# A norm's sums of squares gathered partly by accumulating transfers, and one gate tile from another ring

## The chip, the core and the metric

The kernel runs on one core of one Trainium2 chip. The metric is the device time of one execution in microseconds (us). The engines are named as in the profile: PE multiplies matrices (PEld is its weight load), DVE works elementwise on VectorE, ACT is ScalarE, POOL is GpSimd, which computes nothing here and only issues transfers that add to what lies at the target, and SP issues nearly all other transfers. Each engine runs its instructions in one fixed order and waits on semaphores; an instruction that waits holds up all that stand behind it.

## The reference, cut to what matters

One layer on 1024 tokens of width 1024: a half-weighted SwiGLU, a token mixer with two branches, an output projection, a second half-weighted SwiGLU, a last norm.

```python
h = x + 0.5 * swiglu(rmsnorm(x, norm_ffn1), ffn1_w_in, ffn1_w_out)
proj = rmsnorm(h, norm_mix) @ w_in          # q, k, v, g_ret, p, gates
ret = rms_per_head(retention(q, k, v)) * silu(g_ret)
pool = multiscale_pool(p, pool_w, pool_scale)
gate = sigmoid(gates + gate_bias)
merged = gate[0] * (ret @ w_ret_up) + gate[1] * (pool @ w_pool_up)
h = h + merged @ w_out
h = h + 0.5 * swiglu(rmsnorm(h, norm_ffn2), ffn2_w_in, ffn2_w_out)
return rmsnorm(h, norm_final)
```

The change concerns the sum of h * h over the channels that `rmsnorm(h, norm_ffn2)` needs, and the gates of the pooling branch.

## The kernel before, in words

Activations lie transposed, 128 channels by 1024 tokens in a tile, so that a channel tile `mt` runs from 0 to 7 and a token half `j` from 0 to 1. Each matrix product is done by Strassen's scheme with seven block products (`strassen`, L478), and every operand is split into a high and a low part (`split`, L163): ACT casts the high part (L164), DVE subtracts it (L165), and a block product is three matmuls per 128 channels, high by high (L184), high by low (L185) and low by high (L186). Weights get their parts the same way. So DVE and ACT prepare what PE eats.

Two groups of output tiles run side by side (`two_by_two`, L706), in the order of blocks `BY_OPERAND`: L11 R11, L12 R21, S2 T2, S3 T3, S1 T1, L22 T4, S4 R22. In such a group the product L11 R11 goes to bank `a`; ACT copies `a` to bank `b` (L529) before the second product may go on top of `a` and S2 T2 on top of `b`. These two copies gate PE at the start of each pair of groups.

The stages around the change are: `pool_up` (the pooled branch's up projection, names `pu`, gates `pg`), `two_groups` (the retention branch's, names `ru`, result in operands `mg`), `out_group` (the output projection, names `wo`, with the groups 0 and 1 first and 2 and 3 after them), and the second SwiGLU's input product `ffn_in` (names `c`; its operands are `n3`, made from the results of `out_group`). What PE does not need at once is put on a list, `flow`, of which each step of PE takes two entries; the compiler's scheduler then fixes the order on each engine, with the evacuations of banks (`with soon()`) ahead.

An output tile of `wo` has four quarters. Two of them get the old value of h by an accumulating transfer from POOL (`onto`, L142, called at L1877) after a copy from the bank; the others get it on DVE (L1880, L1882). When a quarter is done, `Next.quarter` (L315) stores it and calls `Norm.square` (L293): ACT squares 128x512 values into a `c2` tile `n3q` (L291), and DVE adds it to `n3ssq` (L303). There are 16 quarters; the first of each token half is squared straight into `n3ssq`, so there are 14 such additions. Then `stats` (L448) has PE sum `n3ssq` over the channels, and the inverse root is made and spread.

`handed` (L1887) says which operand of the next product is made after which block: `f[5]` is the part R22, `f[1]` T2, `f[3]` T3. After the last block of the second pair the rest, for tiles 2 and 3, is put on the list.

SBUF tiles come from rings: `raw` has 4 buffers (weights as loaded, and the pooled gates `pg0` to `pg6`), `tl` 4, `c2` 8 half tiles, `wt` 5 (split weights). A new tile waits until the last reader of its buffer is done; a load waits so on SP, with all later loads behind it.

Of the kernel before, what the change touches and what calls it, by code (L numbers as in the profile page):

```python
# [15 lines left out]
ADD, SUB, MUL = ALU.add, ALU.subtract, ALU.mult  # L16
# [4 lines left out]
KT = D // P  # L21
# [32 lines left out]
BY_OPERAND = (0, 4, 1, 3, 2, 6, 5)  # L54
# [36 lines left out]
def block_kernel(ctx: ExitStack, tc, x, x_tok, x_two, vecs, f1_in, f1_out, w_in, w_v, pool_w, w_ret, w_pool, w_o,  # L91
# [3 lines left out]
    tt = nc.vector.tensor_tensor  # L95
# [4 lines left out]
    flow = Flow()  # L100
# [19 lines left out]
    def raw(name):  # L120
        return sb.tile([P, S], F32, tag="raw", bufs=N_RAW, name=name)

    def tl(name):
        return sb.tile([P, S], F32, tag="tl", bufs=N_TL, name=name)

    def t4(name):
        return sb.tile([P, S], F32, tag="t4", bufs=N_T4, name=name)

    def c2(name):
        return sb.tile([P, H], F32, tag="c2", bufs=N_C2, name=name)  # L130
# [8 lines left out]
    def load(dst, src):  # L139
        nc.sync.dma_start(dst, src)  # L140

    def onto(dst, src):  # L142
        nc.gpsimd.dma_start(dst, src, accum_op=ADD)
# [5 lines left out]
    def spill(name, n, width=S):  # L149
        return [dr.tile([P, width], F32, tag=f"{name}{i}", name=f"{name}{i}") for i in range(n)]  # L150

    def half(t, j):
        return t[:, j * H : (j + 1) * H]
# [126 lines left out]
    class Norm:  # L280


        turns = False

        def __init__(self, name):
            self.name, self.ssq, self.seen = name, None, set()
# [6 lines left out]
        def square(self, mt, tokens, src):  # L293
            if self.ssq is None:
                self.ssq = t4(f"{self.name}ssq")
            dst = self.ssq[:, tokens]
            if tokens.start not in self.seen:
                self.squared(dst, src)
                self.seen.update(range(tokens.start, tokens.stop, HD))
            else:  # L300
                q = c2(f"{self.name}q{mt}_{tokens.start}")[:, : tokens.stop - tokens.start]
                self.squared(q, src)
                tt(dst, dst, q, ADD)  # L303

    class Next(Norm):

        turns = True
# [398 lines left out]
    def two_by_two(groups, order, between=None):  # L706

        groups = list(groups)
        for z in range(0, len(groups), 2):
            pair = [g() for g in groups[z : z + 2]]  # L710
            for n in order:
                a, b = (steps[n] for steps in pair)
                yield a

                def both(b=b, z=z, n=n):
                    b[1]()
                    if between:
                        between(z // 2, n)

                yield b[0], both  # L720


    def plain(M, nk, src, name, evac, begin, banks):

        t = {}
        for q in range(0, nk, 4):

            def prep(q=q):
                if q == 0:
                    t["raw"] = raw(f"{name}raw")  # L730
                    load(t["raw"][:, : nk * P], src)
                t[q] = weights(t["raw"][:, q * P : (q + 4) * P], f"{name}w{q}")
                if q + 4 == nk:
                    begin()

            def body(q=q):
                if q == 0:
                    t["dst"] = [f(f"{name}d{j}") for j, f in enumerate(banks)]
                for i in range(4):
                    w = parts(t[q], i)  # L740
                    m = [moving(M(q + i)[j]) for j in range(2)]
                    first, final = q + i == 0, q + i == nk - 1
                    for j in range(2):
                        mm(t["dst"][j], w[0], m[j][0], start=first, stop=False)
                        mm(t["dst"][j], w[0], m[j][1], start=False, stop=False)
                    for j in range(2):
                        mm(t["dst"][j], w[1], m[j][0], start=False, stop=final)
                if q + 4 == nk:
                    evac(t["dst"])

            yield prep, body
# [434 lines left out]
    def await_stored(*names):  # L1186
        flow.until(lambda: stored.issuperset(names))
# [283 lines left out]
    def pool_up():  # L1471
        gate, stores = {}, {}
        for mt in range(KT):

            def begin(mt=mt):
                await_stored(f"t{(KT + mt) // 2}")
                if mt < KT - 1:
                    r = raw(f"pg{mt}")
                    load(r, gates[KT + mt])
                    gate[mt] = [half(r, j) for j in range(2)]  # L1480
                    stores[mt] = [(pm[mt], r)]
                    return
                gate[mt] = [c2(f"pg{mt}{j}") for j in range(2)]
                for j, g in enumerate(gate[mt]):
                    load(g, half(gates[KT + mt], j))
                stores[mt] = [(half(pm[mt], j), g) for j, g in enumerate(gate[mt])]

            def evac(dst, mt=mt):
                for j, g in enumerate(gate.pop(mt)):
                    tt(g, dst[j], g, MUL)  # L1490
                for to, at in stores.pop(mt):
                    load(to, at)

            yield from plain(M.get, KT, w_pool[mt], f"pu{mt}", evac, begin,
                             (sum_bank, sum_bank if mt < 4 else bank))
# [304 lines left out]
    def after(nx):  # L1800

        def t2(i):
            if i not in nx.t1s:
                nx.r22(i)
            nx.t2(i)

        return {0: nx.r11, 4: nx.r21, 1: t2, 3: nx.t3, 2: nx.t1, 6: nx.t4_, 5: nx.p22}
# [43 lines left out]

        return [group(n, i) for n, i in enumerate(at)]

    waiting = []

    def out_group(i):
        pair = [None, None]
        name = f"wo{i}"

        def begin():  # L1860
            for z in range(2):
                pair[z] = t4(f"{name}{z}")
                if i > 1 or z == 0:
                    load(half(pair[z], 1 - z), half(h1[i + 4 * z], 1 - z))
                else:
                    load(pair[z], h1[i + 4 * z])

        def evac(which, in0, in1):
            tile, j = which
            dst = half(pair[tile], j)  # L1870
            step = lambda: ffn2.quarter(i + 4 * tile, slice(j * H, (j + 1) * H), pair[tile])
            if tile == j and (i > 1 or tile == 0):
                if in1 is not None:
                    tt(dst, in0, in1, ADD)
                else:
                    copy(dst, in0)
                onto(dst, half(h1[i + 4 * tile], j))  # L1877
                waiting.append(step)
                return
            tt(dst, in0, dst, ADD)  # L1880
            if in1 is not None:
                tt(dst, dst, in1, ADD)  # L1882
            flow.add(step)

        return lambda: strassen(mg, w_o[i], w_o[i + 4], name, evac, none, begin)

    def handed(nx, last):  # L1887

        f = after(nx)

        def between(pair, n):
            if n in (3, 5):
                flow.add(*waiting)
                waiting.clear()
            if pair == 0:
                if n == BY_OPERAND[-1]:
                    flow.add(*(lambda m=m, i=i: m(i) for i in range(2) for m in (nx.r22, nx.sum1, nx.sum3)))
                return
            flow.add(*(lambda i=i: f[n](i) for i in range(2)))

            for m in {3: (0,), 6: (4,)}.get(n, ()):
                flow.add(*(lambda i=i: f[m](i) for i in range(2, 4)))
            if n == BY_OPERAND[-1]:
                rest = [lambda m=m, i=i: f[m](i) for m in (1, 3, 2, 6, 5) for i in range(2, 4)]
                last(rest)

        return between

    def merge():
        yield from two_by_two(two_groups(0) + two_groups(1), BY_OPERAND, handed(mg, lambda rest: flow.add(*rest)))  # L1910
        yield from two_by_two((out_group(i) for i in range(4)), BY_OPERAND,
                              handed(ffn2, lambda rest: (flow.add(*rest[:4]), ffn2.stats(between=rest[4:]))))

    ffn2 = Next("n3", V_FFN2, h2)
    ops2 = spill("r2", FH), spill("t2", FH), spill("b2", FH), spill("m2", FH, H)

    class Last(Norm):


        tiles, rows, banks, sums = {}, {}, {}, {}  # L1920
# [87 lines left out]
    def second():  # L2008
        for n, step in enumerate(ffn_in(ffn2, f2_in, ops2, "c", lambda: fetch_rows(f2_out, "d"))):
            flow.rate = 1  # L2010
            yield step
        flow.rate = 2
    flow.run(chain(ffn1(), projections(), retention(), merge(), second(),
                   ffn_out(ffn2, ops2, ops_done.setdefault("c", set()), f2_out, h2, "d", fin.quarter, fin.end, fetched, fin, f2_far)))
    flow.some(-1)
# [95 lines left out]
```

## Time and profile before

| | us |
|---|---|
| median of 3 runs (2061.41 to 2063.96) | 2062.12 |
| the profiled execution, device time | 2062.72 |
| its span, first to last instruction | 2060.9 |
| PE busy | 2040.5 |
| DVE busy | 1831.2 |
| ACT busy | 1092.5 |
| POOL busy | 9.1 |

The profiled execution lies 0.6 us above the median. Its granted TensorE clock was 0.999 over the span. Rows of the timeline give start, duration, engine, line, operation, output and inputs, the count, and in brackets the idle time ahead of it with what ended it; a row can merge a few like instructions. Start times count from the span's start. Line numbers of the profile are those of the kernel before; those of the changed kernel have the same numbers up to L299, numbers 2 higher up to L1852 and 14 to 21 higher behind it.

### The profile page before, as it was taken

The page shows a single profiled execution, that of the slowest core. Times are in us where ns is not written, and L with a number is a line of the kernel's source. Part 1 is how long each engine was busy: PE and PEld are TensorE (multiplying, and loading weights), DVE is VectorE, ACT ScalarE, POOL GpSimd, SP SyncE. Part 2 cuts the span into 40 slices and gives each one's busy share as a digit, 9 for nine tenths or more (in the row PEclk, how much of TensorE's full clock was granted, in tenths as well). Part 3 has the DMA queues.
Part 4 walks back from the last instruction along what each step waited for, and adds up shares of the span by engine and source line. Part 5 has one row for each costly group of instructions (what it writes and reads, how often), then busy time and mean ns, then how long its engine had stood idle before and what let it go on. Part 6 is the DMA issues. An engine that isn't in the chain of part 4 may idle for free.

```text
span 2060.9 us, 29728 instructions
## 1 busy us (share of the span) xinstructions
PE 2040.5 (99%) x10672; PEld 1810.4 (88%) x10672; DVE 1831.2 (89%) x3253; ACT 1092.5 (53%) x2066; POOL 9.1 (0%) x14
## 2 busy tenths in 40 slices
PE   9999999999999999999999999999999999999998
PEld 7888999988888888888888999888889989998887
DVE  8889998998996798989789987899989989899896
ACT  8545454554754554454447753456645545455454
POOL 0000000000000000000000000010000000000000
PEclk9999999999999999999999999999999999999999
DMA  6332424585543333243337667545223232368642
GB/s 245 137 103 77 143 88 143 199 274 196 187 146 109 107 136 110 85 151 119 117 125 229 203 227 278 185 109 163 82 98 133 88 133 88 135 208 274 211 148 97
DMA packets 120260, 313.57 MB, mean 152 GB/s; under 512 B 13361, under 2 KB 17585, under 8 KB 120113
## 3 DMA queue, kind: packets, MB, share of 16 engines
q1 hardware_dynamic: 118096, 308.01, 43.9%
q0 software_dynamic: 1440, 2.62, 0.8%
q8 instruction: 83, 1.36, 0.3%
q10 hardware_dynamic: 576, 1.05, 0.1%
q14 instruction: 65, 0.52, 0.1%
HBM read 220.93 MB, written 90.70 MB: 151 GB/s over the span
## 4 chain that ended last, share of the span: by engine, by line
PE 81%; DVE 12%; DMA 2%; ACT 2%; issue 2%; SPq 0%; ACTq 0%; DVEq 0%
PE c_b L185 2%; PE c_b L184 2%; PE c_b L186 2%; PE a_b L184 2%; PE a_b L186 2%; PE a_b L185 2%; PE c_e L186 2%; PE c_e L184 2%; PE c_e L185 2%; PE a_e L186 1%; PE a_e L184 1%; PE a_e L185 1%; PE a_a L186 1%; PE a_a L185 1%; PE a_a L184 1%
## 5 line engine op out<-in xcount | busy, mean ns | idle before, releaser
L184 PE MATMUL c_b<-n3T,c_wS 128*128 128x512 f32 x176 | 66.8, 380 | 1.7 <-ACT n3T L164 1.7
L185 PE MATMUL c_b<-n3T,c_wS 128*128 128x512 f32 x176 | 66.8, 380 | 0.0
L186 PE MATMUL c_b<-n3T,c_wS 128*128 128x512 f32 x176 | 66.7, 379 | 0.0
L184 PE MATMUL a_b<-n1T,a_wS 128*128 128x512 f32 x168 | 63.7, 379 | 0.0
L185 PE MATMUL a_b<-n1T,a_wS 128*128 128x512 f32 x168 | 63.7, 379 | 0.0
L186 PE MATMUL a_b<-n1T,a_wS 128*128 128x512 f32 x168 | 63.7, 379 | 0.0
L184 PE MATMUL a_a<-n1R,a_wL 128*128 128x512 f32 x120 | 45.5, 379 | 0.0
L186 PE MATMUL a_a<-n1R,a_wL 128*128 128x512 f32 x120 | 45.5, 379 | 0.0
L185 PE MATMUL a_a<-n1R,a_wL 128*128 128x512 f32 x120 | 45.5, 379 | 0.0
L184 PE MATMUL c_a<-n3R,c_wL 128*128 128x512 f32 x112 | 42.7, 381 | 0.7 <-ACT c_b L529 0.5
L185 PE MATMUL c_a<-n3R,c_wL 128*128 128x512 f32 x112 | 42.4, 379 | 0.0
L186 PE MATMUL c_a<-n3R,c_wL 128*128 128x512 f32 x112 | 42.4, 379 | 0.0
L184 PEld LDWEIGHTS c_b<-n3T,c_wS 128*128 128x128 f32 x176 | 33.3, 189 | 6.6 <-ACT n3T L164 2.1
L185 PEld LDWEIGHTS c_b<-n3T,c_wS 128*128 128x128 f32 x176 | 33.3, 189 | 4.8 <-DVE n3T L165 0.3
L186 PEld LDWEIGHTS c_b<-n3T,c_wS 128*128 128x128 f32 x176 | 33.3, 189 | 4.7
L186 PEld LDWEIGHTS a_b<-n1T,a_wS 128*128 128x128 f32 x168 | 31.8, 189 | 4.5
L185 PEld LDWEIGHTS a_b<-n1T,a_wS 128*128 128x128 f32 x168 | 31.8, 189 | 4.4
L184 PEld LDWEIGHTS a_b<-n1T,a_wS 128*128 128x128 f32 x168 | 31.8, 189 | 4.4
L165 DVE TENSOR_TENSOR a_wS<-a_S,a_wS 128x512 fp32r<-128x512 f32 x45 | 30.7, 684 | 3.8 <-ACT a_wS L164 3.8
L165 DVE TENSOR_TENSOR c_wS<-c_S,c_wS 128x512 fp32r<-128x512 f32 x46 | 31.2, 681 | 2.6 <-ACT c_wS L164 2.6
L164 ACT CAST a_wS<-a_S 128x512 fp32r<-128x512 f32 x45 | 27.3, 621 | 11.7 <-PE a_a L186 6.1
L184 PE MATMUL c_e<-n3T,c_wS 128*128 128x512 f32 x88 | 33.5, 380 | 0.0
(3167 smaller groups left out, 8012.2 us busy)
## 6 DMA issues: line engine op xcount, KB each, us to landing
c_ra<-in_f_in SPq DMA_DIRECT2D x22, 512.0 KB, 3.6
c_rb<-in_f_in SPq DMA_DIRECT2D x22, 512.0 KB, 3.5
a_ra<-in_f_in SPq DMA_DIRECT2D x21, 512.0 KB, 3.7
a_rb<-in_f_in SPq DMA_DIRECT2D x21, 512.0 KB, 3.7
t<-au SPq DMA_DIRECT2D x11, 512.0 KB, 3.5
b<-ag SPq DMA_DIRECT2D x11, 512.0 KB, 4.1
r<-au SPq DMA_DIRECT2D x11, 512.0 KB, 3.7
bra<-in_f_out SPq DMA_DIRECT2D x11, 512.0 KB, 5.5
```

The source lines that it names most:

```text
L164: copy(hi, src)
L165: tt(lo, src, hi.bitcast(F32), SUB)
L184: mm(dst, w[0], m[0], start=start, stop=False, skip_group_check=True)
L185: mm(dst, w[0], m[1], start=False, stop=False, skip_group_check=True)
L186: mm(dst, w[1], m[0], start=False, stop=stop, skip_group_check=True)
```

## The change

Four things are edited. `ffn2`, the norm of the second SwiGLU, gets a hook `apart` for the 14 additions. The hook takes half of a `tl` tile in place of a `c2` tile for the square, and then issues an accumulating transfer on POOL onto `n3ssq` for 8 of the quarters, while 6 others are put on a list `sums` that is worked off by DVE later, after the first four entries of `rest` (`settled`). In `handed`, for both norms that use it, the operand `f[5]` of tiles 0 and 1 is no longer asked for ahead of the rest but behind T2 and T3 of tiles 2 and 3. And the gate tile `pg6` comes from the ring `tl` in place of `raw`.

```diff
+            elif self.aside:
+                self.aside(mt, tokens, dst, src)
...
-                    r = raw(f"pg{mt}")
+                    r = (tl if mt == KT - 2 else raw)(f"pg{mt}")
...
+    def apart(mt, tokens, dst, src):
+
+        if not spare:
+            q = tl(f"n3q{mt}_{tokens.start}")
+            spare.extend((half(q, 1), half(q, 0)))
+        q = spare.pop()
+        ffn2.squared(q, src)
+        if mt % 4 < 2 or mt < 4 and not tokens.start:
+            onto(dst, q)
+        else:
+            sums.append(lambda: tt(dst, dst, q, ADD))
...
+            if pair and n == BY_OPERAND[-1]:
+                rest = [lambda m=m, i=i: f[m](i) for m, at in ((1, 2), (3, 2), (5, 0), (2, 2), (6, 2), (5, 2))
+                        for i in (at, at + 1)]
+                last(rest)
+                return
...
-            if n == BY_OPERAND[-1]:
-                rest = [lambda m=m, i=i: f[m](i) for m in (1, 3, 2, 6, 5) for i in range(2, 4)]
-                last(rest)
...
+    def settled(rest):
+
+        flow.add(*rest[:4], lambda: [f() for f in sums[:3]], lambda: [f() for f in sums[3:]])
+        ffn2.stats(between=rest[4:])
...
-                              handed(ffn2, lambda rest: (flow.add(*rest[:4]), ffn2.stats(between=rest[4:]))))
+                              handed(ffn2, settled))
...
+    ffn2.aside = apart
```

PE's own order stays, but for the sums of `n3ssq`, which stand some 18 matmuls later. Three places show what moves on the other engines.

First place, the start of `out_group`'s first pair. On DVE, before, from the low part of the weights `wo0wS2` to that of `wo1wS2` (`mgt` and `ru` with `mgT2`, `mgT3` are the sums for T2 and T3; `wo1S` those of the weights):

```order
L165 TENSOR_TENSOR wo0wS2_13645<-wo0S2_13643,wo0wS2_13645 128x512
L351 TENSOR_TENSOR ru20_13292<-ru21_13294,mgt12_13667 128x512
L351 TENSOR_TENSOR ru30_13328<-ru31_13330,mgt13_13673 128x512
L492 TENSOR_TENSOR wo1S1_13679<-wo1rb_13563 128x512
L165 TENSOR_TENSOR mgT22_13670<-ru20_13292,mgT22_13670 128x512
L165 TENSOR_TENSOR mgT23_13676<-ru30_13328,mgT23_13676 128x512
L492 TENSOR_TENSOR wo1S2_13681<-wo1S1_13679,wo1ra_13562 128x512
L351 TENSOR_TENSOR ru20_13292<-ru21_13294,ru20_13292 128x512
L351 TENSOR_TENSOR ru30_13328<-ru31_13330,ru30_13328 128x512
L165 TENSOR_TENSOR wo1wS2_13683<-wo1S2_13681,wo1wS2_13683 128x512
```

The same stretch of DVE in the changed kernel:

```order
L165 TENSOR_TENSOR wo0wS2_13651<-wo0S2_13649,wo0wS2_13651 128x512
L165 TENSOR_TENSOR mgT32_13674<-ru20_13292,mgT32_13674 128x512
L353 TENSOR_TENSOR ru30_13328<-ru31_13330,ru30_13328 128x512
L494 TENSOR_TENSOR wo1S1_13681<-wo1rb_13563 128x512
L507 TENSOR_TENSOR wo0rb_13540<-wo0ra_13539,wo0rb_13540 128x512
L165 TENSOR_TENSOR mgT33_13678<-ru30_13328,mgT33_13678 128x512
L494 TENSOR_TENSOR wo1S2_13683<-wo1S1_13681,wo1ra_13562 128x512
L165 TENSOR_TENSOR mgR220_13707<-ru01_12942,mgR220_13707 128x512
L165 TENSOR_TENSOR mgR221_13710<-ru11_12985,mgR221_13710 128x512
L165 TENSOR_TENSOR mgT12_13731<-mgt12_13635,mgT12_13731 128x512
L165 TENSOR_TENSOR wo1wS2_13685<-wo1S2_13683,wo1wS2_13685 128x512
```

The operands T2 and T3 and the parts `mgR22` have changed places with the weights' sums. Counted from DVE's `ru30<-ru30,ru3h01` (L1845), which has the same place in both kernels, `wo1wS2` is the 15th instruction behind it before and the 19th now.

On ACT at the same place, before:

```order
L1876 COPY wo00_13648<-wo0a_13652 128x512
L164 CAST wo1wS2_13683<-wo1S2_13681 128x512
L164 CAST mgT32_13706<-ru20_13292 128x512
L164 CAST mgT33_13710<-ru30_13328 128x512
L1876 COPY wo10_13686<-wo1a_13690 128x512
L164 CAST mgT12_13731<-mgt12_13667 128x512
L164 CAST mgT13_13734<-mgt13_13673 128x512
L291 ACTIVATE n3ssq_13840<-wo00_13648 128x512
L164 CAST wo0wS3_13714<-wo0rb_13540 128x512
L534 COPY wo0v_13778<-wo0b_13665 128x512
L164 CAST wo1wS3_13738<-wo1rb_13563 128x512
```

And now:

```order
L164 CAST mgT33_13678<-ru30_13328 128x512
L164 CAST mgR220_13707<-ru01_12942 128x512
L164 CAST mgR221_13710<-ru11_12985 128x512
L164 CAST mgT12_13731<-mgt12_13635 128x512
L164 CAST mgT13_13734<-mgt13_13641 128x512
L1890 COPY wo10_13688<-wo1a_13692 128x512
L164 CAST wo1wS2_13685<-wo1S2_13683 128x512
L164 CAST wo0wS3_13714<-wo0rb_13540 128x512
L291 ACTIVATE n3ssq_13840<-wo00_13654 128x512
L536 COPY wo0v_13778<-wo0b_13671 128x512
L291 ACTIVATE n3q1_0_13843<-wo10_13688 128x512
L164 CAST wo1wS3_13738<-wo1rb_13563 128x512
```

The cast of `wo1wS2` now stands behind the copy of the quarter `wo10`, and the square of that quarter, which needs its residual by transfer, stands ahead of the cast of `wo1wS3`.

Second place, ACT at the start of the second SwiGLU (`c0_b` is the copy that PE needs for the second product of `c0`; `n3R`, `n3T` are operands, `wo20` to `wo31` the quarters of the last two output groups). Before:

```order
L168 ACTIVATE n3R213_14376<-wo31_14017,vec_66 128x512
L164 CAST n3R220_14427<-wo01_13650 128x512
L164 CAST n3R221_14430<-wo11_13688 128x512
L164 CAST c0_wS2_14312<-c0_S2_14310 128x512
L529 COPY c0_b_14328<-c0_a_14315 128x512
```

And now:

```order
L168 ACTIVATE n3R213_14369<-wo31_14014,vec_66 128x512
L291 ACTIVATE n3q2_512_14378<-wo20_13983 128x512
L291 ACTIVATE n3q6_512_14410<-wo21_13985 128x512
L291 ACTIVATE n3q6_512_14410<-wo31_14014 128x512
L164 CAST c0_wS2_14305<-c0_S2_14303 128x512
L348 ACTIVATE wo21_13985<-wo21_13985,vec_66 128x512
L291 ACTIVATE n3q2_512_14378<-wo30_14012 128x512
L348 ACTIVATE wo31_14014<-wo31_14014,vec_66 128x512
L164 CAST n3T22_14418<-wo20_13983 128x512
L531 COPY c0_b_14321<-c0_a_14308 128x512
```

All four last squares, the two scalings in place and a cast that needs DVE's result stand ahead of the copy now.

Third place, POOL from the first output group on, before:

```order
L143 DMA wo00_13648<-h10_168 128x512
L143 DMA wo10_13686<-h11_169 128x512
L143 DMA wo20_13986<-h12_170 128x512
L143 DMA wo30_14015<-h13_171 128x512
L143 DMA wo21_13988<-h16_174 128x512
L143 DMA wo31_14017<-h17_175 128x512
```

And now:

```order
L143 DMA wo00_13654<-h10_168 128x512
L143 DMA wo10_13688<-h11_169 128x512
L143 DMA n3ssq_13840<-n3q1_0_13843 128x512 x2
L143 DMA n3ssq_13840<-n3q4_0_13909 128x512 x2
L143 DMA n3ssq_13840<-n3q0_512_13953 128x512 x2
L143 DMA wo20_13983<-h12_170 128x512
L143 DMA wo30_14012<-h13_171 128x512
L143 DMA n3ssq_13840<-n3q2_0_14162 128x512 x2
L143 DMA wo21_13985<-h16_174 128x512
L143 DMA wo31_14014<-h17_175 128x512
```

Six of the new transfers stand ahead of the residuals of the third and fourth output group, and two ahead of their last ones. Transfers onto the same half of `n3ssq` wait for one another.

More of the change, by code (lines that the diff above doesn't have):

```diff
@@ L280, in block_kernel @@
     class Norm:
-        turns = False
+        turns, aside = False, None
         def __init__(self, name):
@@ L1852, in two_groups @@
         return [group(n, i) for n, i in enumerate(at)]
-    waiting = []
+    waiting, sums, spare = [], [], []
+    def apart(mt, tokens, dst, src):
[8 more added lines that the diff above has]
+            sums.append(lambda: tt(dst, dst, q, ADD))
     def out_group(i):
```

## The prediction

> **What bounds the kernel now.** I read the page first, then what PE waited for between 1290 and 1530 us, where all edited instructions lie, and then the timeline of PE, ACT, DVE and POOL around each of these waits. The page:
>
> ```profile
> span 2060.9 us, 29728 instructions
> PE 2040.5 (99%) x10672; PEld 1810.4 (88%) x10672; DVE 1831.2 (89%) x3253; ACT 1092.5 (53%) x2066; POOL 9.1 (0%) x14
> ```
>
> PE is busy for all but 20.4 us of the span, and the change takes no matmul away. It can only take away, or add, idle time of PE. The waits of PE in the stretch:
>
> ```profile
> PE ru1a L184 <- ACT ru1b L529: 1.8, 1, 1.8
> PE c_b L184 <- ACT n3T L164: 1.7, 1, 1.7
> PE wo2a L184 <- ACT wo2b L529: 1.3, 1, 1.3
> PE c_a L184 <- ACT c_b L529: 0.5, 1, 0.5
> PE c_y L184 <- ACT n3R L164: 0.4, 1, 0.4
> PE wo0e L186 <- DVE wo0wS L165: 0.2, 1, 0.2
> ```
>
> They sum to 5.9 us. That is the most that the change can gain, 0.29% of the time. A measurement of this kernel can tell about 0.2%, or 4.1 us, from no change. The stages say why each wait is there:
>
> ```profile
> core 0: us, PE busy (x) PEld busy (x) DVE busy (x) ACT busy (x) POOL busy (x), PEclk, DMA share, GB/s
> 1380.00:1400.00 20.00, 19.82 (x92) 16.94 (x91) 20.00 (x34) 15.25 (x28) 1.74 (x2) 1.00 0.50 133
> 1400.00:1420.00 20.00, 18.65 (x87) 16.02 (x86) 17.51 (x29) 10.92 (x18) 0.00 (x0) 1.00 0.47 178
> 1440.00:1460.00 20.00, 19.34 (x89) 16.31 (x88) 19.00 (x32) 11.86 (x21) 1.74 (x2) 1.00 0.39 106
> ```
>
> DVE is full or nearly so, the clock is at 1.00, ACT is half idle but waits for DVE in its fixed order. So PE's gaps come from DVE's row of work, through ACT.
>
> **The change part by part.** What it removes:
>
> ```profile
> L303 DVE TENSOR_TENSOR n3ssq<-n3ssq,n3q x14: 679/685/694, 1399.8 to 1461.6; 128x512 f32<-128x512 f32 x14
> ```
>
> Eight of these 14 leave DVE: 8 x 0.685 = 5.5 us of busy time, a little less in the row, since starts follow each other every 0.60 us. None of it is PE's time by itself. The six others stay. What follows for PE I work out wait by wait, in order of time.
>
> *The ring of `pg6`.* The wait of 1.8 us at `ru1a` ends with this chain:
>
> ```profile
> 1288.02 0.33 SPq L140 DMA_DIRECT2D ru1ra<-in_w_ret  x1
> 1297.54 0.33 SPq L140 DMA_DIRECT2D ru1rb<-in_w_ret  x1
> 1301.85 0.69 DVE L492 TENSOR_TENSOR ru1S<-ru1rb 128x512 f32<-128x512 f32 x1 [1.13 <-DMA ru1rb<-in_w_ret]
> 1308.47 0.68 DVE L390 TENSOR_TENSOR ret<-ret,ret 128x512 f32<-128x512 f32 x1
> 1309.67 0.68 DVE L390 TENSOR_TENSOR ret<-ret,ret 128x512 f32<-128x512 f32 x1
> 1309.71 0.58 ACT L529 COPY ru1b<-ru1a 128x512 f32<-128x512 f32 x1
> ```
>
> With `pg6` out of `raw`, `ru1rb` can take the buffer that `ru1ra` took, so it is asked for near 1288.0 instead of 1297.5, and DVE's 1.13 us go. But the new order on ACT puts the casts of both first `ret` results ahead of the copy `ru1b`, where one stood, and so the copy now needs the second L390 row. That row would end at 1309.67 - 1.13 + 0.68 = 1309.22, against the first one's 1309.15 before. One cast (0.5) lies between in both. The gain is spent on the spot: 0 for this part; bounds -0.1 and, if the earlier load is slow because others run beside it, +0.7.
>
> *The first output pair.* The rows:
>
> ```profile
> 1378.03 0.68 DVE L1845 TENSOR_TENSOR ru<-ru,ru3h 128x512 f32<-128x512 f32 x1
> 1387.19 0.69 DVE L165 TENSOR_TENSOR wo1wS<-wo1S,wo1wS 128x512 fp32r<-128x512 f32 x1
> 1387.83 0.58 ACT L1876 COPY wo<-wo1a 128x512 f32<-128x512 f32 x1
> 1388.14 0.38 PE L184 MATMUL wo1b<-mgT,wo1wS 128*128 128x512 f32 x1
> ```
>
> `wo1wS` was the 15th row behind the first of these, 9.16 us or 0.61 each; as the 19th it starts at 1378.03 + 11.5 = 1389.5 and ends at 1390.2. PE's third matmul of `wo1b` wants it two matmuls behind the first, which at 19.82 / 92 = 0.215 each is 1388.6. Nothing covers that: a new wait of 1.5 us. ACT agrees, since its cast of the high part now stands behind the copy of 1387.83 and ends near 1389.1. The copy for `wo0a` also slips behind a cast, for 0.2. The 0.4 us that PE lost at `wo0e` (0.2 idle, and as much in the restart) go, since PE now comes later. Sum: +1.3.
>
> *The second output pair.* PE waited here for a copy that stood behind squares:
>
> ```profile
> 1417.99 0.58 ACT L529 COPY wo2b<-wo2a 128x512 f32<-128x512 f32 x1
> 1418.63 0.48 PE L184 MATMUL wo2a<-mgR,wo2wL 128*128 128x512 f32 x1 [1.35 <-ACT wo2b L529]
> ```
>
> PE lost 1.35 idle and some 0.2 in the restart, so it was ready at 1417.1. Six additions leave DVE ahead of this point, and with them most of this idle time:
>
> ```profile
> L303 DVE TENSOR_TENSOR n3ssq<-n3ssq,n3q 128x512 f32<-128x512 f32 x10 | 6.9, 689 | 2.6 <-ACT n3q L291 2.6
> ```
>
> But the squares still stand ahead of the copy on ACT, with weights' casts between them. So I don't move the copy: it ends at 1418.57 in the row above, and I give it 0.7 either way. PE now comes 1.3 later, at 1418.4, so 0 to 0.9 is lost of the former 1.55. I take -1.4, and +0.1 for the cast that now stands ahead of the second such copy.
>
> *The start of the second SwiGLU.* The rows:
>
> ```profile
> 1453.14 0.68 DVE L1880 TENSOR_TENSOR wo<-wo3b,wo 128x512 f32<-128x512 f32 x1
> 1455.05 0.58 ACT L529 COPY c_b<-c_a 128x512 f32<-128x512 f32 x1
> 1455.57 0.74 ACT L291 ACTIVATE n3q<-wo 128x512 f32<-128x512 f32 x1
> 1455.69 0.48 PE L184 MATMUL c_a<-n3R,c_wL 128*128 128x512 f32 x1 [0.53 <-ACT c_b L529]
> 1464.74 0.62 ACT L164 CAST n3T<-wo 128x512 fp32r<-128x512 f32 x1 [1.71 <-DVE wo L353]
> 1378.03:1453.14 75.11, 71.59 (x118) 1.00 0.51 151
> ```
>
> In the new order the copy `c0_b` stands behind all four last squares and the cast of `n3T22`, so it follows DVE's `wo<-wo3b`. That row is 116 rows behind 1378.03 before and 113 now (of the ten additions above one is left, and six rows for the weights of `c` have moved ahead). At 71.59 / 116 = 0.617 each, 113 are 69.7 us. DVE's idle time in the stretch was 75.11 - 71.59 = 3.5. It grows where a square on ACT waits for a residual with a weight's cast behind it. The first such place can be priced:
>
> ```profile
> 1388.77 0.86 POOL L143 DMA_DIRECT2D wo<-h  x1 [2.74 <-ACT wo L1876]
> 1389.24 4.35 SPq L140 DMA_DIRECT2D h<-wo  x2
> wo<-h POOLq DMA_DIRECT2D x6, 256.0 KB, 4.0
> ```
>
> The residual of `wo10` was issued at 1388.77, and the store that waits for it ended at 1393.59, so it landed near 1393.3. The square then ends at 1394.1, the cast of `wo1wS3` behind it at 1394.7, and DVE, for which it is the 25th row behind 1378.03, is there at 1393.1 and idles 1.6. There are two or three more such places, for the third and fourth group. I take 6 us of idle time in all, bounds 2 and 7. So `wo<-wo3b` starts at 1378.0 + 69.7 + 6.0 = 1453.7, bounds 1450.0 (PE's product ends then) and 1454.7. Behind it DVE has two rows and a subtraction (0.6 x 3 + 0.7), then come cast and copy (0.5 + 0.6): the copy ends 3.7 later, at 1457.4. PE, in step by then, wants it at 1455.0: a wait of 2.4, bounds 0 and 3.5. The old losses here, 0.5 and 0.1 after the copies, go: +1.8. The wait of 1.7 at `c_b` goes as well, since the operand's cast now stands ahead of PE's start: -1.7.
>
> The Trainium skill (DMA: Bandwidth & Descriptors, "Anatomy of one DMA") fits a POOL transfer as 2.0 us and its bytes at 436 GB/s, an estimate of 2.6 us for 256 KB. The rows above show 4.0 and about 4.5 here; by the page's figure the residual would be there 1.4 to 1.9 us earlier, the idle time would shrink, and the sum would come out some 1.5 lower. The measurement decides.
>
> *The new transfers* cost POOL 0.86 of issue each, as in the row of 1388.77, 8 x 0.86 = 6.9 us on an engine that is idle. Their landing is hidden: the last four additions on a half end before the six of DVE, and PE's sum stands later.
>
> Sum: 0 + 1.3 - 1.3 + 1.8 - 1.7 = +0.1 us on 2062.72, or 2062.8 for the profiled execution; it lies 0.6 above the median, so **2062.2** for the median.
>
> **The rivals.** *The copies are not late.* If ACT finds the last results of DVE as early as PE allows, the wait at `c0_b` is 0, and the sum falls by 2.4 to -2.3: 2059.8. For it speaks that DVE has 5 us less to do, against it that the order shows the copy behind four squares. If also the first stage's wait of 1.8 and the new one of 1.5 stayed away, 2056.6 would come out; the rows of 1309.67 and 1387.19 speak against both. Chance 0.22, of it 0.04 for more than 4.1.
>
> *POOL becomes the path* (slower). The residuals of `wo20` and `wo30` stand behind six accumulates, of which those on one half run one after another, and the third to sixth can start only as their squares end, from about the time of the first row here:
>
> ```profile
> 1411.09 0.75 ACT L291 ACTIVATE n3q<-wo 128x512 f32<-128x512 f32 x1 [0.85 <-DVE wo L1882]
> 1423.44 0.86 POOL L143 DMA_DIRECT2D wo<-h  x1 [33.81 <-ACT wo L1876]
> 1431.38 0.62 ACT L164 CAST wo2wL<-wo2rb 128x512 fp32r<-128x512 f32 x1
> 1439.45 0.38 PE L184 MATMUL wo2e<-mgT,wo2wL 128*128 128x512 f32 x1
> ```
>
> At 4.1 us each they are issued at 1411.2, 1415.4, 1416.3 and 1420.5, and POOL is free at 1421.4, ahead of the 1423.44 at which the residual of `wo20` was issued. All ten accumulates of the trace read DRAM; one from SBUF isn't there. Bounds are 2, half of the row, and 8, twice it. At 8 they are issued at 1411.2, 1419.2, 1420.1 and 1428.1, and the residual lands near 1437, 9.6 later than the 1427.4 of before. The square that waits for it holds up ACT's weights `wo2wL`, which had 8 us to spare before PE and have some 5 in the new order, with the residual's square ahead. PE loses 4.6: 2066.8. It decides from about 5.6 us per accumulate. Against it speaks that the nearest rows, all six of `wo`, are at 4.0. Chance 0.18, half of it for more than 4.1.
>
> The Trainium skill (SBUF — State Buffer, "Who interferes with whom") knows a way to this: POOL's descriptors wait while DVE holds a shared port, 0.62 us becoming 3.1 in its example. It gives that for one-input operations in a faster mode and infers that two-input ones don't do it; here the issue took 0.86 beside a full DVE, which is no starved issue.
>
> *It does nothing* because cover hides all of it, new waits as well: then only the old waits stay, 2062.1. It falls in the forecast's range and is counted there.
>
> **How the numbers follow.** The forecast, old waits exchanged for new ones with a sum between -1.5 and +2.5, has 0.60; 2062.2 is its time. The range takes in the first rival's -2.3 and the high ends of the terms (0.7 above the ring's 0, 0.8 above the second pair's -1.3, 1.1 above the 2.4 at `c_a`), with 0.4 at the high end for the runs' scatter: 2059.7 to 2065.2. Faster by over 0.2% needs nearly all six waits gone: 0.04. Slower by over 0.2% is the second rival's far end: 0.09. The rest, 0.87, is within 0.2%.
>
> **What would show it.** Right: PE's waits list a wait near 1388 at `wo1b` of 1 to 1.6 us, none at `c_b` for `n3T`, one at `c_a` for `c_b` of over 1 us, and still one near 1.8 at `ru1a`; POOL shows 18 issues of 0.9. Wrong: no wait at `wo1b`, a wait at `wo2b` or `wo2e` for weights (POOL late), or DVE's idle time for squares below 2 us with `c_a` on time.

## The result, and the profile after

The changed kernel took 2070.74 us (median of 6 runs, 2069.43 to 2072.26), the kernel before on the same chip 2063.64 (6 runs, 2061.41 to 2064.47): the ratio is 1.0037, with a 95% interval of 1.0026 to 1.0047. By the ratio that is 7.6 us slower (the medians lie 7.1 us apart), where 2062.2 had been forecast with a range up to 2065.2. The profiled execution took 2072.26 us, 1.5 above its median.

The page of the changed kernel first:

```profile
span 2070.5 us, 29748 instructions
PE 2046.1 (99%) x10672; PEld 1813.0 (88%) x10672; DVE 1827.9 (88%) x3245; ACT 1092.7 (53%) x2066; POOL 16.1 (1%) x22
```

DVE has lost 3.3 us of work and POOL has gained 8 instructions and 7 us, as the change says. Yet PE's busy time has grown by 5.6 us with the same 10672 matmuls. A stretch of slower matmuls at the third place below accounts for 2.6 us of it; the rest was not followed up. What PE waited for from 1200 to 1600 us (in total, how often, the longest):

```profile
PE c_a L184 <- ACT c_b L531: 4.6, 1, 4.6
PE wo1e L184 <- ACT wo1wS L164: 1.7, 1, 1.7
PE ru1a L184 <- ACT ru1b L531: 0.7, 1, 0.7
PE wo1b L184 <- ACT wo1wS L164: 0.6, 1, 0.6
PE wo2b L184 <- DVE wo L1888: 0.5, 1, 0.5
...
PE wo1b L186 <- DVE wo1wS L165: 0.4, 1, 0.4
PE c_y L184 <- ACT n3R L164: 0.4, 1, 0.4
PE wo3b L184 <- ACT wo3v L536: 0.3, 1, 0.3
PE wo2a L184 <- ACT wo2b L531: 0.2, 1, 0.2
```

The wait at `c_b` is gone and those at `ru1a` and `wo2a` have shrunk; in their place stand one of 4.6 us at `c_a`, one of 1.7 at `wo1e` and several small ones. To see where the time is lost, take the first matmuls of `wo0a`, `wo2a`, `c_a` and `c_x` from PE's timeline, before:

```profile
1375.19 0.38 PE L184 MATMUL wo0a<-mgR,wo0wL 128*128 128x512 f32 x1
1411.93 0.38 PE L184 MATMUL wo2a<-mgR,wo2wL 128*128 128x512 f32 x1
1449.81 0.38 PE L184 MATMUL c_a<-n3R,c_wL 128*128 128x512 f32 x1
1518.02 0.27 PE L184 MATMUL c_x<-n3R,c_wx 128*128 128x256 f32 x1
```

and after:

```profile
1376.52 0.38 PE L184 MATMUL wo0a<-mgR,wo0wL 128*128 128x512 f32 x1
1416.77 0.38 PE L184 MATMUL wo2a<-mgR,wo2wL 128*128 128x512 f32 x1
1455.06 0.38 PE L184 MATMUL c_a<-n3R,c_wL 128*128 128x512 f32 x1
1527.49 0.27 PE L184 MATMUL c_x<-n3R,c_wx 128*128 128x256 f32 x1
```

The first output pair takes 40.3 us instead of 36.7, the second 38.3 instead of 37.9, the start of the second SwiGLU 72.4 instead of 68.2. Together that is 151.0 against 142.8, 8.1 us more, about the whole difference between the two kernels. (The two profiled executions lie 9.5 us apart; the other 1.4 us arise ahead of `wo0a`.) From `ru0a`'s first matmul to `wo0a`'s it takes 73.4 instead of 74.6, but this piece moved between 72.5 and 74.7 in ten of the eleven runs below, whatever was edited, and took 76.7 in the eleventh. It follows PE's wait at `ru1a`: without that wait 72.5 to 72.9 us are left in each of the ten. Of the 8.1 us, 1.3 is the wait at `wo1b`, as the run with R22 later alone will show. Three places make the rest.

**First place.** The timeline of POOL, SP, ACT, DVE and PE around `wo1e` after the change:

```profile
1390.24 0.86 POOL L143 DMA_DIRECT2D wo<-h  x1 [3.27 <-ACT wo L1890]
1390.35 0.32 SPq L140 DMA_DIRECT2D h<-wo  x1
1390.77 0.37 SPq L140 DMA_DIRECT2D wo<-h  x1
1396.94 0.74 ACT L291 ACTIVATE n3q<-wo 128x512 f32<-128x512 f32 x1 [4.90 <-DMA wo<-h]
1398.22 0.69 DVE L165 TENSOR_TENSOR wo1wS<-wo1rb,wo1wS 128x512 fp32r<-128x512 f32 x1 [3.73 <-ACT wo1wS L164]
1398.25 0.48 PE L184 MATMUL wo1e<-mgT,wo1wS 128*128 128x512 f32 x1 [1.69 <-ACT wo1wS L164]
```

ACT stands 4.90 us in front of the square of `wo10`, which needs the residual that POOL issued at 1390.24 and that landed 6.7 us later. Behind the square stands a cast of weights; DVE idles 3.73 us for it and PE 1.69. The row on SP points at why the residual was slow: the load of `wo11`, 512 KB (the row `wo<-h` at 1390.77), was issued 0.5 us behind it. Before, SP had these rows:

```profile
1363.32 15.14 SPq L140 DMA_DIRECT2D wo<-h  x3
1389.24 0.32 SPq L140 DMA_DIRECT2D h<-wo  x1
```

The load of `wo11` was the third of the first row, at 1378.1, ahead of the stores; now it stands behind the store of `wo00` on SP.

**Second place.** The same engines around the residual of `wo30`:

```profile
1432.07 0.87 POOL L143 DMA_DIRECT2D wo<-h  x1 [3.44 <-ACT wo L1890]
1432.90 0.37 SPq L140 DMA_DIRECT2D c_rb<-in_f_in  x1
1433.63 0.87 POOL L143 DMA_DIRECT2D n3ssq<-n3q  x1 [0.70 <-ACT n3q L291]
1438.78 0.75 ACT L291 ACTIVATE n3q<-wo 128x512 f32<-128x512 f32 x1 [3.52 <-DMA wo<-h]
1440.17 1.41 DVE L169 SCALAR_TENSOR_TENSOR n3R<-wo,vec,n3R 128x512 fp32r<-128x512 f32 x2 [3.84 <-ACT n3R L168]
```

Again a square on ACT waits for a residual that took 6.7 us, with a load of 512 KB issued 0.8 us behind it and here an accumulating transfer as well, 1.6 us behind it. DVE idles 3.84 us.

**Third place.** ACT, DVE and PE at the start of the second SwiGLU, and PE's clock by stage (the last three numbers of a row of windows are the granted clock, the DMA share and GB/s):

```profile
1459.59 2.00 ACT L291 ACTIVATE n3q<-wo 128x512 f32<-128x512 f32 x3
1460.99 0.68 DVE L1894 TENSOR_TENSOR wo<-wo3b,wo 128x512 f32<-128x512 f32 x1
1462.63 0.73 ACT L291 ACTIVATE n3q<-wo 128x512 f32<-128x512 f32 x1
1464.38 0.57 ACT L531 COPY c_b<-c_a 128x512 f32<-128x512 f32 x1
1465.01 0.80 PE L184 MATMUL c_a<-n3R,c_wL 128*128 128x512 f32 x1 [4.60 <-ACT c_b L531]
```

```profile
1379.36:1460.99 81.63, 77.38 (x348) 64.63 (x346) 70.50 (x114) 49.75 (x89) 12.25 (x14) 1.00 0.63 165
1465.00:1470.20 5.20, 5.19 (x12) 4.20 (x13) 5.06 (x9) 3.72 (x7) 0.00 (x0) 0.50 0.00 0
```

The copy `c0_b` (the row `c_b<-c_a`) stands behind four squares, as the order said, and DVE reaches `wo<-wo3b` only at 1460.99: from the same row as in the prediction's count it was idle 81.63 - 70.50 = 11.1 us. ACT, once DVE lets it go on at 1457.81, has no idle time up to the copy, so the squares' own time on ACT counts here as well. PE waits 4.60 us, and then the granted clock is 0.50: for 5.2 us each matmul takes 0.43 us instead of 0.216, which costs another 2.6 us.

### The profile page after: what moved, and what is told of

It reads as the page before. It is cut to its first block, busy times and chain, and to the rows that moved or that the text cites. A ratio compares the mean times of both kernels' runs of the same rounds, so it can differ in the third digit from the quotient of the medians.

```text
span 2070.5 us, 29748 instructions
## 1 busy us (share of the span) xinstructions
PE 2046.1 (99%) x10672; PEld 1813.0 (88%) x10672; DVE 1827.9 (88%) x3245; ACT 1092.7 (53%) x2066; POOL 16.1 (1%) x22
## 5 line engine op out<-in xcount | busy, mean ns | idle before, releaser
L184 PE MATMUL c_e<-n3T,c_wL 128*128 128x512 f32 x88 | 33.4, 380 | 0.0
```

Of the source, the lines that this page charges most:

```text
L184: mm(dst, w[0], m[0], start=start, stop=False, skip_group_check=True)
```

## The experiments

Three theories were put against each other. **Theory one:** the squares cost the time. They lie in `tl` tiles now and stand further ahead on ACT, where they wait for residuals with casts and copies behind them. (That the scheduler moves them ahead because `tl` tiles come free earlier than `c2` tiles is argued; the runs show only that the ring decides the place.) **Theory two:** the accumulating transfers themselves cost it. **Theory three:** asking for R22 later costs it. In the table, the ratio is to the kernel before on the same chip, "PE" the time from `wo0a`'s first matmul to the first `c_x`, the waits are PE's in us, and the residuals' columns give the us from issue to landing (all from the one profiled execution of each run).

| run | ratio, 95% interval | PE, us | `wo1b` | `wo1e` | `c_a`, longest | residual `wo10` | `wo30` |
|---|---|---|---|---|---|---|---|
| before | 1 | 142.8 | 0 | 0 | 0.5 | 4.5 | 3.9 |
| changed | 1.0037 (1.0026 to 1.0047) | 151.0 | 1.0 | 1.7 | 4.6 | 6.7 | 6.7 |
| ring alone | 1.0004 (0.9995 to 1.0012) | 143.3 | 0 | 0 | 0.5 | 4.6 | 5.0 |
| R22 later alone | 1.0003 (0.9994 to 1.0012) | 143.0 | 1.0 | 0 | 0.5 | 5.8 | 3.9 |
| hook alone | 1.0032 (1.0020 to 1.0044) | 147.7 | 0 | 0.7 | 4.5 | 4.6 | 6.6 |
| squares in `c2` | 1.0006 (0.9997 to 1.0015) | 141.5 | 1.0 | 0 | 0 | 6.1 | 4.0 |
| late squares in `c2` | 1.0022 (1.0012 to 1.0031) | 146.2 | 1.0 | 0.6 | 0.9 | 5.6 | 6.3 |
| fill, 20 matmuls | 1.0034 (1.0021 to 1.0046) | 148.7 | 1.0 | 1.1 | 0.3 | 6.1 | 6.3 |
| eight on DVE | 1.0019 (1.0010 to 1.0027) | 146.1 | 1.0 | 0.8 | 1.6 | 5.7 | 4.7 |
| `c2`, R22 for one norm | 0.9999 (0.9990 to 1.0008) | 142.1 | 0 | 0 | 0.9 | 4.5 | 4.1 |
| six transfers | 1.0042 (1.0027 to 1.0057) | 149.8 | 1.0 | 1.0 | 5.3 | 6.0 | 6.2 |
| fill, 7 matmuls | 1.0047 (1.0031 to 1.0063) | 151.8 | 1.0 | 1.1 | 3.1 | 6.1 | 6.6 |
| R22 for one norm alone | 1.0004 (0.9995 to 1.0013) | 143.5 | 0 | 0 | 0.5 | 4.6 | 4.0 |

**The ring alone.** In this and the next three runs, "the stretch" is PE's time from `ru0a`'s first matmul to the first `c_a` of the second pair of groups: 228.3 us before, 235.3 in the changed kernel. The kernel before, with

```diff
-                    r = raw(f"pg{mt}")
+                    r = (tl if mt == KT - 2 else raw)(f"pg{mt}")
```

> Only the gate tile in the other ring. The stretch of PE from its first matmul of ru0a to the first c_a of the second pair of groups took 228.3 us before and 235.3 after. If the squares' place on ACT costs the time (theory one): the weights' load ru1rb is asked for early, DVE's stall of 1.1 us goes, the stretch is 227.1 to 228.3 and the time within 2 us of before. If the accumulating transfers cost it (theory two) or the later operand R22 does (theory three): the same, so this run only splits off the ring.

The stretch was 227.8 us, and the time is not told apart from before. The ring accounts for neither a loss nor a gain that can be told.

**R22 later alone.** The kernel before, with the reordered `rest` in `handed` for both norms:

```diff
+            if pair and n == BY_OPERAND[-1]:
+                rest = [lambda m=m, i=i: f[m](i) for m, at in ((1, 2), (3, 2), (5, 0), (2, 2), (6, 2), (5, 2))
+                        for i in (at, at + 1)]
+                last(rest)
+                return
...
-            if n == BY_OPERAND[-1]:
-                rest = [lambda m=m, i=i: f[m](i) for m in (1, 3, 2, 6, 5) for i in range(2, 4)]
-                last(rest)
```

> Only the operand R22 asked for later. Theory one (squares ahead on ACT): a wait of 1.0 to 1.5 us at wo1b, none at wo1e because the square of wo10 stands behind the weights here, no wait over 1 us at c_a, and a stretch of 227.5 to 229.5 against 228.3. Theory two (accumulating transfers): the same. Theory three (this reorder is the cause): a stretch of 232 to 235, with waits at wo1b, wo1e and c_a.

The wait at `wo1b` is there, 0.6 and 0.4 us, and no other new one over 0.5; the first output pair takes 38.0 us instead of 36.7. The stretch is 226.4, even 1 us under the expected range because the wait at `ru1a` is missing, and the time is that of before. Theory three falls. The residual of `wo10` took 5.8 us here as well, since this edit alone already puts the load of `wo11` behind the store; but the square of `wo10` stands late on ACT, so nothing waits for it.

**The hook alone.** The kernel before, with `apart`, `settled` and the transfers, without ring and reorder. Against the changed kernel that is:

```diff
-                    r = (tl if mt == KT - 2 else raw)(f"pg{mt}")
+                    r = raw(f"pg{mt}")
...
-            if pair and n == BY_OPERAND[-1]:
-                rest = [lambda m=m, i=i: f[m](i) for m, at in ((1, 2), (3, 2), (5, 0), (2, 2), (6, 2), (5, 2))
-                        for i in (at, at + 1)]
-                last(rest)
-                return
...
+            if n == BY_OPERAND[-1]:
+                rest = [lambda m=m, i=i: f[m](i) for m in (1, 3, 2, 6, 5) for i in range(2, 4)]
+                last(rest)
```

> Only the hook for the additions: squares in half tl tiles, eight transfers, six late sums. Theory one: no wait at wo1b; the load of wo11 again ahead of the stores, so the residual of wo10 lands in about 4.5 us and the wait at wo1e is under 0.7; copy c0_b behind the squares, a wait of 3 to 5 us at c_a with about 2.5 us of half clock behind it, stretch 231 to 235. Theory two (transfers): a similar stretch, but with residuals of wo landing at 6 us or more at wo10 as well. Theory three: 228 or less.

Its rows at the first place, and PE's two largest waits:

```profile
1388.28 0.86 POOL L143 DMA_DIRECT2D wo<-h  x1 [2.74 <-ACT wo L1890]
1392.87 0.75 ACT L291 ACTIVATE n3q<-wo 128x512 f32<-128x512 f32 x1 [2.25 <-DMA wo<-h]
1394.15 0.69 DVE L165 TENSOR_TENSOR wo1wS<-wo1rb,wo1wS 128x512 fp32r<-128x512 f32 x1 [1.34 <-ACT wo1wS L164]
```

```profile
PE c_a L184 <- ACT c_b L531: 4.5, 1, 4.5
PE wo1e L184 <- ACT wo1wS L164: 0.7, 1, 0.7
```

Most of the loss, 6.6 us by the ratio, comes with the hook. The square stands as far ahead as in the changed kernel, but with the load of `wo11` back ahead of the stores the residual is there after 4.6 us, DVE idles 1.34 us instead of 3.73, and PE waits 0.7 instead of 1.7 at `wo1e`. So the first place needs both edits: the hook puts the square ahead, and the later R22 puts the load beside what it waits for. The stretch is 231.4, 3.1 more than before.

**All squares in `c2` tiles.** The changed kernel, with

```diff
-        if not spare:
-            q = tl(f"n3q{mt}_{tokens.start}")
-            spare.extend((half(q, 1), half(q, 0)))
-        q = spare.pop()
+        q = c2(f"n3q{mt}_{tokens.start}")
```

> The changed kernel with one edit: the squares lie in c2 tiles as before, so they stand late on ACT again; the eight transfers, the late sums, the later R22 and the ring stay. Theory one: a wait of 1.0 to 1.5 us at wo1b, none at wo1e, under 1.5 us at c_a, full clock throughout, stretch 226.5 to 229.5. Theory two (the transfers cost it): stretch 232 or more, with POOL or residuals late at wo2. Theory three (R22 later): 232 or more, with waits at wo1e and c_a.

PE's largest waits in it:

```profile
PE ru1a L184 <- ACT ru1b L531: 1.9, 1, 1.9
PE c_b L184 <- ACT n3T L164: 0.9, 1, 0.9
PE wo1b L184 <- ACT wo1wS L164: 0.6, 1, 0.6
```

All eight transfers are still there, and the loss is gone: the stretch is 227.0, 1.3 less than before, and the time is that of before. With the smaller ring the squares stand late on ACT again, `c0_b` ahead of the last four, and the loads `c0_ra` and `c0_rb` behind both stores on SP. Theory two falls, theory one stands.

**Only the late squares in `c2` tiles.** The changed kernel, with

```diff
+        moved = mt % 4 < 2 or mt < 4 and not tokens.start
-        if not spare:
+        if moved and not spare:
...
-        q = spare.pop()
+        q = spare.pop() if moved else c2(f"n3q{mt}_{tokens.start}")
```

> The changed kernel, but the six squares whose additions come late lie in c2 tiles, so that on ACT the last four stand behind the copy c0_b again; the eight squares that are added by transfer stay in tl tiles and ahead. The stretch of PE from ru0a's first matmul to the first c_x took 217.5 us before, 224.4 after. If the last squares ahead of the copy make the wait at c_a (theory one): that wait is under 1 us, no half clock, the waits at wo1b, wo1e, wo2b and wo3b stay, stretch 219.5 to 221.5, time 3 to 5 us below the changed kernel. If the copy is late because DVE is late by then (theory two): still over 3 us at c_a, or the same time lost at c_b for n3T, stretch 223 or more.

PE waits 0.9 us at most at `c_a`, at full clock, while the first and second place remain in kind: the two residuals take 5.6 and 6.3 us, DVE idles 2.64 and 3.77 us for them, and PE waits 0.6 us at `wo1e`; the waits at `wo2b` and `wo3b`, which had been expected to stay, are not there. The stretch, from here on from `ru0a`'s first matmul to the first `c_x` (217.5 us before, 224.4 in the changed kernel), is 220.1, and the time is 3 us below the changed kernel's by the ratios, whose intervals overlap a little. So DVE's lateness alone does not make the third place; it needs the four squares ahead of the copy.

**Twenty matmuls in the wait.** The changed kernel, with products that nobody reads, ahead of the product that waits:

```diff
             prod("a", "L11", "R11", True, False)
+            if name == "c11_":
+                d = bank("fill")
+                for k in range(FILL):
+                    mm(d, parts(t["w", "L11"], k % 4)[0], moving(nx.operand("R11", k % 4))[0], start=k == 0,
+                       stop=k == FILL - 1, skip_group_check=True)
```

> The changed kernel with 20 more matmuls into a bank that nobody reads, between the first products of the second SwiGLU and the product that waits for c0_b; the order on ACT, DVE, SP and POOL is the same. If the half clock behind the wait at c_a comes from PE's idle time (theory one): the 20 take 4.3 us of the wait, about 0.4 us of it is left, the matmuls behind it keep 0.216 us, the stretch is 221.3 to 222.5 against 224.4, the time 2 to 3 us below the changed kernel. If those matmuls are slow for a reason of their own, such as the load on memory or the operands (theory two): again some 12 matmuls at 0.43 us, stretch 224 to 225.

PE's rows at the place, and the window behind it:

```profile
1458.61 4.48 PE L533 MATMUL fill<-n3R,c_wL 128*128 128x512 f32 x20
1463.40 0.48 PE L185 MATMUL c_a<-n3R,c_wL 128*128 128x512 f32 x1 [0.32 <-ACT c_b L537]
```

```profile
1463.30:1468.00 4.70, 4.60 (x21) 4.06 (x22) 4.54 (x8) 3.76 (x9) 0.00 (x0) 1.00 0.00 0
```

The clock stays at 1.00, and the part from `c_a` to `c_x` is 69.9 us instead of 72.4: the half clock comes from PE's own idle time and costs 2.6 us. The stretch to `c_x` is 221.9, as theory one said. The median's ratio, 1.0034, does not tell this gain from none.

**The eight additions on DVE.** The changed kernel, with

```diff
-            onto(dst, q)
+            tt(dst, dst, q, ADD)
```

> The changed kernel with the eight additions on DVE at once instead of by transfer, the squares still in tl tiles and ahead on ACT. Theory one (the squares' place costs it, the transfers don't): waits at wo1e and c_a as in the changed kernel, DVE eight rows of 0.6 us fuller, stretch 223 to 228. Theory two (the transfers cost it): residuals of wo land in 4.0 to 4.6 us, the waits at wo1e and c_a go, stretch 219 or less.

Neither expectation held: the stretch is 220.4, faster than the changed kernel and slower than before. The wait at `wo1e` is 0.8, with the residual of `wo10` at 5.7 us; but without the transfers the scheduler put `c0_rb` behind the store of `wo30` on SP, the residual of `wo30` was there after 4.7 us, and DVE's 3.84 us of the second place are gone. PE waits 1.6 us at `c_a`, at full clock, and with eight more rows on DVE it waits 2.0 us at `wo2a` and 1.3 at `wo3a`. This run leaves open whether the transfer or the load slowed the residual of `wo30`; the next run but one answers that.

**The squares in `c2` tiles, R22 later for one norm.** The run with all squares in `c2` tiles, with one more edit:

```diff
-            if pair and n == BY_OPERAND[-1]:
+            if nx is ffn2 and pair and n == BY_OPERAND[-1]:
...
+            if n == BY_OPERAND[-1]:
+                rest = [lambda m=m, i=i: f[m](i) for m in (1, 3, 2, 6, 5) for i in range(2, 4)]
+                last(rest)
```

> The changed kernel with all squares in c2 tiles and the later R22 for the second norm alone, so that the operands of the output projection are made in the order of before. Theory one: no wait at wo1b, none at wo1e, under 1 us at c_a, stretch 214.5 to 216.5 against 217.5 of before; the time 0 to 3 us below before, which the measurement may not tell from none. If the late additions and transfers cost something that the stretch does not show: 2 us or more above before.

No wait is left at `wo1b` and `wo1e`; the stretch is 216.7, a little over the expected range, PE needs 142.1 us from `wo0a` to `c_x`, 0.7 less than before, and the time is not told apart from before.

**Six transfers.** The changed kernel, with

```diff
-        if mt % 4 < 2 or mt < 4 and not tokens.start:
+        if mt % 4 < 2:
```

> The changed kernel, but the squares of wo20 and wo30 are added late by DVE as well, so six transfers are left and none is issued near the residual of wo30; ACT's order and the load c0_rb, issued just behind that residual, stay. The residual landed after 6.7 us in the changed kernel, 3.9 before. If the load of 512 KB beside it is what slows it (theory one): again over 6 us, DVE idle for about 3.8 us behind the square, the wait at c_a over 3.5 us with half clock. If the accumulating transfer issued 1.6 us behind it does (theory two): under 5 us, DVE idle for under 2 us, the wait at c_a 2 us or more shorter and no half clock.

```profile
1431.54 0.87 POOL L143 DMA_DIRECT2D wo<-h  x1 [3.50 <-ACT wo L1890]
1432.34 0.37 SPq L140 DMA_DIRECT2D c_rb<-in_f_in  x1
1437.77 0.74 ACT L291 ACTIVATE n3q<-wo 128x512 f32<-128x512 f32 x1 [3.06 <-DMA wo<-h]
```

With no accumulating transfer beside it the residual of `wo30` still takes 6.2 us; the load of 512 KB issued 0.8 us behind it is enough. DVE idles 3.4 us, PE waits 5.3 us at `c_a`, and the half clock is there again, for 7 matmuls. Theory one's reading of the second place holds.

**Seven matmuls in the wait.** The run with the fill, with 7 in place of 20:

> The changed kernel with 7 matmuls for nobody in place of the 20 ahead of the product that waits for c0_b: they take 1.5 us of the wait, so PE idles for about 3 to 3.4 us there. Waits up to 2.0 us left the clock at 1.00 in the runs so far, waits of 4.5 and 4.6 us halved it. If the halving needs an idle time between these two sizes that lies over 3.4 us: full clock, 0.216 us behind the wait. If it lies below 3 us: 5 to 12 matmuls at 0.43 us. Either is open; no theory of the main question hangs on it.

PE's first matmul behind the wait, and the window from there:

```profile
1469.74 0.79 PE L185 MATMUL c_a<-n3R,c_wL 128*128 128x512 f32 x1 [3.10 <-ACT c_b L537]
```

```profile
1469.70:1475.00 5.30, 5.26 (x12) 4.16 (x13) 5.16 (x9) 4.36 (x9) 0.00 (x0) 0.50 0.00 0
```

An idle time of 3.1 us halves the clock too, for 13 matmuls. The same trace shows a shorter wait that did so, at `ru1a`:

```profile
1314.07 0.48 PE L185 MATMUL ru1a<-ruR,ru1wL 128*128 128x512 f32 x1 [2.20 <-ACT ru1b L537]
1315.32 0.63 PE L187 MATMUL ru1a<-ruR,ru1wL 128*128 128x512 f32 x1
1317.88 0.63 PE L187 MATMUL ru1a<-ruR,ru1wL 128*128 128x512 f32 x1
```

After 2.2 us of waiting the first matmuls ran at full speed, and from 1315.32 on 7 followed each other every 0.43 us. This wait and the slower matmuls behind it are why the piece from `ru0a` to `wo0a` took 76.7 us in this run. With waits of 1.92 us (`wo2a` in the next run) and 1.95 us (`wo2a` with the additions on DVE) the clock stayed full. So in these traces waits below 2 us left the clock alone, and one of 2.2 us did not.

**R22 later for one norm alone.** The kernel before, with the reorder for the second norm only (`nx is ffn2`), no hook and no ring:

> The kernel before with one edit: the second norm alone asks for its operand R22 later; no additions are moved, no ring is changed. If the additions that leave DVE bring nothing by themselves (theory one): no wait at wo1b or wo1e, PE from wo0a's first matmul to the first c_x in 141.5 to 142.9 us against 142.8 before and 142.1 with the additions moved in c2 tiles, the time within 2 us of before. If they are worth something: over 1 us longer in this stretch than with them.

From `wo0a` to `c_x` it took 143.5 us, 1.4 more than with the additions moved in `c2` tiles, with the wait at `wo2a` (1.9 us) back. So, by one profile each, the additions that leave DVE are worth a little over 1 us in this stretch; the ratios, 1.0004 and 0.9999, do not show it.

## Why the prediction was wrong, point by point

- **What bounds the kernel** held: only PE's waits moved the time. But "they sum to 5.9 us; that is the most that the change can gain" has no counterpart on the other side, and the loss was larger than any gain could be.
- **The ring**, 0 forecast: no effect was found. The wait at `ru1a` came out at 0.7 us and not near 1.8. PE began `ru0a` 2.5 us later than in the profile of before, but that does not explain it: in the run with seven matmuls PE began 3.4 us later and waited 2.2. Over the runs this wait lies between none (R22 later alone, the hook alone) and 2.2; it moves by as much without the ring as with it, and why stays open.
- **The first output pair**, +1.3 forecast: right for what it priced. The wait at `wo1b` is 0.6 and 0.4 us, and with R22 later alone, where it is the only new wait of this piece, the piece took 38.0 us instead of 36.7. The runs with the old order of R22 in the first norm lack it. Missed was `wo1e`: with it the piece took 40.3 us, 2.2 more.
- **The second pair**, -1.3: the wait at `wo2a` shrank by 1.0. Missed were `wo3b` and `wo2b`, 0.8 us of idle time and their restarts, behind DVE's second stall, so that the piece came out 0.4 us longer.
- **The wait at `c_b`**, -1.7: gone, as forecast.
- **The failed step** is the fourth, the start of the second SwiGLU, in its sentence "I take 6 us of idle time in all, bounds 2 and 7". DVE idled 11.1 us. The time of the rows was right (69.7 us forecast, 70.5 busy), the last link was right (the copy ended 4.0 us behind `wo<-wo3b`, 3.7 forecast), and the squares with casts behind them were named; but the one residual that was priced got the 4.5 us that it took before, and the other places were taken as alike. Two took 6.7. Had they taken 4.5 and 3.9 as before, 5.0 of the 11.1 us would not have arisen and 6.1 would be left, by an estimate that takes DVE's idle time to shrink with the residual's; the hook alone bears this out at the first place, where a residual of 4.6 us left DVE 1.34 us idle, with 1.6 forecast. So the mechanism held and this term was mis-sized. Their issue on POOL did not change; what changed is what SP issues beside them, and SP's order was never read. The load of `wo11` had slipped behind a store that waits for the first residual, and `c0_rb` had slipped in behind the residual of `wo30`. Over the thirteen kernels of the table the residual of `wo10` took 4.5 to 4.6 us wherever the load of `wo11` stood ahead of the stores, and 5.6 to 6.7 in the eight where it followed. That of `wo30` took 6.2 to 6.7 in the six kernels where `c0_rb` was issued within 0.9 us of it, and 3.9 to 5.0 in the other seven.
- The idle time was followed to `c_a` alone, though the text had DVE late at `wo1wS3` by name; PE waited for exactly that at `wo1e`.
- The wait at `c_a` was forecast as 2.4 us with a bound of 3.5, and was 4.6. **The price of a long wait** was put at nothing: it was 2.6 us of half clock. The Trainium skill has the rule (TensorE: Matmul & The Clock Gate, "Part 1: The HAM clock gate"): after an idle window of about 3.4 us the array runs at half rate until it has been busy for as long. The run with the fill agrees that idle time is the cause; the idle time that was enough here lies below that figure, with 3.1 us at `c_a` and 2.2 at `ru1a`.
- **The slower rival**, POOL as the path, is not what happened, though the kernel did become slower. The residual of `wo20` was issued at 1427.46, within 1 us of its copy, and none of PE's waits at `wo2b` and `wo2e` was for weights, which was its sign; the new accumulates took 3.2 to 5.0 us, and 7.4 only beside `c0_rb`, against the 5.6 from which it was to decide. With the same eight transfers and the squares late, the time was that of before.

## What to carry to other kernels

When an edit frees an instruction from a scarce buffer, a scheduler may put it earlier; if it waits for a transfer, everything behind it on its engine waits too, so look first at which instructions came ahead of the ones PE needs. Price such a transfer by what the other queues issue within a microsecond of it in the new order, and read the order of every queue, also of those that no line of the diff touches. Follow each idle time to every consumer, and add the lost clock to a wait of PE that comes near or above 2 us.

## What the runs showed of the hardware

- PE's waits of 3.1, 4.5, 4.6 and 5.3 us at `c_a` halved the granted clock behind them, for 7 to 13 matmuls of 0.43 us instead of 0.216. A wait of 2.2 us at `ru1a` did so for 7 matmuls, beginning 1.25 us behind the end of the wait. Waits of up to 1.95 us left the clock full, in the stretch from 1200 to 1540 us of all thirteen traces.
- An accumulating transfer of 256 KB from DRAM took 3.7 to 5.4 us with no load of 512 KB issued within 0.9 us of it, and 5.6 to 6.7 with one. From SBUF to SBUF it took 3.2 to 5.0 us in the changed kernel, one of 3.9 among them with such a load issued 0.85 us behind it, and 7.4 when issued 0.7 us behind such a load. In the two runs that put it among four such loads (all squares in `c2` tiles, with R22 later for both norms and for one) it took 8.7 and 8.4.
- POOL's issue of such a transfer stayed at 0.86 to 0.89 us in the changed kernel's output projection, beside a DVE that was busy for 86% of the time (70.5 of 81.6 us), but for one row of 1.17 that began while the issue ahead of it was still running.
